# One decoder block on one core: accumulator tiles of one PSUM bank, the scratch write of a transpose on another queue, input sums and chunks at other places, a table loaded later

## The chip, the core and the metric

The kernel runs on one core of one Trainium2 chip. The core has a matrix engine (TensorE, PE in the profile; its weight loads are PEld), a vector engine (VectorE, DVE), an activation engine (ScalarE, ACT), GpSimd (POOL), and a queue processor that only issues transfers (SyncE, SP). They run side by side and wait for each other through semaphores. Matmuls read SBUF and write into banks of the accumulator memory, PSUM, from which DVE and ACT read. Weights come from device memory by DMA. The metric is the device time of one execution in microseconds (us), lower is better; several executions are timed, and one further execution is recorded by the hardware profiler.

## What is computed

One layer on a sequence of 256 tokens of width 2048, all in float32. Cut to what matters:

```python
def swiglu(x, w_gate, w_up, w_down):
    return (jax.nn.silu(x @ w_gate) * (x @ w_up)) @ w_down      # D_FF = 5632
h = x
h = h + 0.5 * swiglu(rms_norm(h, ffn1_norm), ffn1_w_gate, ffn1_w_up, ffn1_w_down)
n = rms_norm(h, mix_norm)
rq, rk, rv, rg, sq, sk, sv = split(n @ w_in)                    # 8 retention heads, 16/2 window heads
ret = silu(rg) * groupnorm(retention(rope(rq), rope(rk), rv))   # two chunks of 128
swa = sliding_window_attention(rope(sq), rope(sk), sv, sinks)   # window 128
h = h + concat(ret, swa) @ w_out
h = h + memory_cross_attention(rms_norm(h, xa_norm), rms_norm(mem, mem_norm), xa_wq, xa_wkv, xa_wo)
h = h + 0.5 * swiglu(rms_norm(h, ffn2_norm), ffn2_w_gate, ffn2_w_up, ffn2_w_down)
out = rms_norm(h, final_norm)
```

## The kernel before

**Data.** The state `h` is held transposed in four tiles `hT[0..3]`, each 128 partitions by 4 x 256 (block b holds rows 512b to 512b+511 of the width, all 256 tokens). A matmul takes 128 tokens of such a block as the stationary operand and 512 columns of a weight as the moving one. Each float32 value is split into a high and a low part (`halves`, lines 80 to 83: ACT copies the high part, line 78, DVE subtracts it, line 83), and a product is three matmuls (`three`, line 644): high by high, high by low, low by high.

**Weights.** A weight piece is 128 x 1024 float32, 512 KB. `load` (lines 356 to 363) issues its DMA on SP into one of `LAND = 10` landing tiles `wf`. `split` turns it into `wh` and `wl`, of which there are four each. A landing tile is free when both halves are made; SP works through its queue in order, and a load whose landing tile is not free yet holds up everything behind it.

**The order of the work** is written out by hand. `all_steps` makes one list. A plain step multiplies one weight piece with one block: two row groups of six matmuls, 12 in all. `run_stream` goes through the list: before a step it runs what has come due (`later(delay, fn)` counts in steps through `clock`; a chunk counts half), splits the pieces of up to `LOOKAHEAD = 3` steps ahead and issues loads of four more. Instructions of due tasks are pinned behind what was issued before them on PE, ACT and DVE; SP keeps the written order throughout.

**Two kinds of unit.** A `Unit` is one 512-column block of a weight, with one accumulator of two banks (`ps_acc`, two tiles of 128 x 2 x 512, one bank for each group of 128 tokens). A `Twin` does two such blocks (gate and up of one feed-forward block b, or two blocks of the down projection). For some of its input blocks (`sevens`: block 3, and also block 2 where b is even; in a down projection the first block of its group) it uses seven products in place of eight, called P1 to P7: six matmuls each, here a chunk. For these the weights are combined first (`prepare`: a subtraction on DVE, line 237, for P5, P6, P7 and P4), and for P5, P6, P3 and P7 so are the inputs (`sums_of`: four scalings on ACT, four additions or subtractions on DVE, line 292, then a split). After the last P1, P5, P6 and P7 the Twin's partial sums are copied from PSUM by ACT and added by DVE (`keep`, `keep_other`, `middle`, `spread`; line 255). Twins take their four banks from the pool `ps_tmp` (four tiles of one bank) and from `ps_acc` (two tiles of two banks) by turns, the first of each feed-forward from `ps_tmp`. The chunks of a Twin lie between the plain steps of the Twin before it; only the first Twin of each feed-forward, b = 1, has none before it, and puts P1, P5, P6, P3, P2, P7 in one row ahead of its own plain steps. `multiply` of any chunk is put into the program after the input sums (`run_until`, line 476).

**First block.** Block b = 0 of each feed-forward is two Units, gate and up. In the first one, the 16 steps of both are interleaved and loaded ahead (`FIRST = 16`). `gate_done` (line 686), when the gate's last step is through, applies Silu and registers the input sums of block 3 (one step later) and block 2 (eight steps later).

**Norms.** `Norm.stat` squares and adds a block; `finish`, `delay` steps after the last block, adds the two halves (line 573), sums over partitions with four tiny matmuls (line 576) and takes the power on GpSimd (line 579).

**Transposes.** `cross` (lines 611 to 630) transposes 32 x 32 squares on DVE into a tile `t4k` (line 618; there are two), writes it to scratch memory `box` with one DMA on SP (line 622, 512 KB), reads it back in four DMAs on GpSimd's queue (line 627, 128 KB each), and `delay` steps later (6 and more) its consumer is put into the program. 64 of these run in all.

**Tables.** `ctab` holds cosines, sines and masks (512 KB) in a tile of its own; it and `sinks` are loaded at step 24. `dmat` takes two landing tiles when the first of the four blocks of the first feed-forward's output is complete (`near_mix`).

Of the kernel before, what the change touches and what calls it, by code (L numbers as in the profile page):

```python
# [34 lines left out]
FIRST = 16  # L35
TURN = 6
SWA_EVERY = 5
LAND = 10
# [5 lines left out]
def decoder_block(ctx: ExitStack, tc: tile.TileContext, a: dict, out: bass.AP):  # L44
# [7 lines left out]
    ps_acc = ctx.enter_context(tc.tile_pool(name="ps_acc", bufs=2, space=bass.MemoryType.PSUM))  # L52
# [17 lines left out]

    def tmp_ps(dt=F32):
        return ps_tmp.tile([P, 512], dt, tag="tmp", name=nm("tmp"))
# [15 lines left out]
    ctab = const.tile([P, C_END], F32, tag="ctab", name="ctab")  # L88
# [94 lines left out]
    class Twin:  # L183
# [16 lines left out]
        def __init__(self, weights, lhs, plain, sevens, sums, done, ahead=False, spare=False):  # L200
            self.w, self.lhs, self.plain, self.sevens = weights, lhs, list(plain), list(sevens)
            self.sums, self.done, self.ahead, self.spare = sums, done, ahead, spare
            self.acc, self.tiles = {}, {}
# [120 lines left out]
    def all_steps():  # L324
        groups = []
        rest = list(units)
        while rest:
# [55 lines left out]
    def run_stream():  # L383
        steps = all_steps()
        steps[:FIRST] = [x for y in zip(steps[: FIRST // 2], steps[FIRST // 2 : FIRST]) for x in y]
        steps[1], steps[2] = steps[2], steps[1]
        loaded, ahead = {}, [FIRST]
        for i in range(0, FIRST, 4):
            if i == 0:
                load_x(0, 0, 2)  # L390
                loaded[0] = loaded[1] = [load(steps[0][0].w[f], 0) for f in range(2)]
                load_x(0, 2, 4)
            else:
                load_x(i // 4, 0, 4)
            for at in range(max(i, 2), i + 4):
                loaded[at] = load(steps[at][0].w, steps[at][3])
# [32 lines left out]
        def multiply_first(u, x, parts, orders):  # L429

            for f, lo, hi in orders:
                for k in range(lo, hi):
                    for t in range(2):
# [3 lines left out]
                            u.acc[t][:, t, f * S : (f + 1) * S], x[:, k, 0, ts], x[:, k, 1, ts], wh, wl,  # L437
# [24 lines left out]
        for at, (u, b, ks, which, first, last) in enumerate(steps):  # L462
# [25 lines left out]
            if first:  # L488
                u.acc = [ps_acc.tile([P, 2, 512], F32, tag="acc", name=nm("acc"))] * 2
                if u.per_half:  # L490
                    u.acc[1] = ps_acc.tile([P, 2, 512], F32, tag="acc", name=nm("acc"))
# [3 lines left out]
            else:  # L495
                for t in range(2):
                    y = (u.acc[t][:, t, : u.n], x, wh, wl, ks, t, first, last)
# [5 lines left out]
            if last:  # L503
                if u.per_half:
                    u.done(u.acc[0], 0)
                    for y in held:
                        by_tokens(*y)
                    u.done(u.acc[1], 1)
                else:
                    u.done(u.acc[0])  # L510
# [100 lines left out]
    def cross(src, then, delay=TURN):  # L611
# [9 lines left out]
        def write():  # L621
            nc.sync.dma_start(box.rearrange("(t p) n -> p t n", t=2), z)
# [24 lines left out]
    def to_h(w, lhs, factor, blocks, norm=None, then=None, spare=0, seven=None, sums=None):  # L647
# [18 lines left out]
        for b in range(4):  # L666
            if seven is None:
                Unit(w, b, 512, lhs, lambda acc, b=b: done([acc[:, t, :] for t in range(2)], b), blocks, pair=True)
# [6 lines left out]
    twins = []  # L675
# [5 lines left out]
    def ffn(norm, w_gate, w_up, down, groups):  # L681
# [4 lines left out]
        def gate_done(b, acc):  # L686
# [29 lines left out]
        twins.clear()  # L716
        starts = [x[0] for x in groups[:2]]
        for g, fbs in enumerate(groups):
            for b in fbs:
# [6 lines left out]
                for f, w in enumerate((w_gate, w_up)):  # L726
                    Unit(w, b, 512, norm.blocks, lambda acc, f=f, done=done: done(f, [acc[:, t, :] for t in range(2)]), range(4), pair=True)
# [588 lines left out]
```

## Time and profile before

| | |
|---|---|
| median of 3 runs | 2197.73 us (2191.67 to 2197.75) |
| profiled execution | 2193.53 us |
| its span, first to last instruction | 2191.7 us |
| mean granted TensorE clock | 0.994 |
| VectorE busy | 1673.9 us, 76% |
| ScalarE busy | 1210.9 us, 55% |
| GpSimd busy | 160.2 us, 7% |
| moved by DMA | 482.62 MB, mean 220 GB/s |

"Busy" is the time in which an engine has an instruction of the program in work; matmuls overlap, so a busy PE is not one at its peak. An engine's wait is put down to the instruction that released it last. The granted clock is the share of full speed at which TensorE was let run.

### The profile page before, as it was taken

The numbers are of one execution on the slowest core, as the hardware profiler recorded it, in microseconds if no ns is written. First come the engines' busy times: TensorE is split into PE (matmuls) and PEld (weight loads), VectorE is DVE, ScalarE is ACT, GpSimd is POOL, SyncE is SP. The second block draws the span as 40 slices with busy tenths as digits, with TensorE's granted clock in tenths as the row PEclk, the third lists the DMA queues.
The fourth block names the chain that finished last, engine by engine and source line by source line (L and its number), as shares of the span: only waits on it lengthen the run. The fifth ranks groups of instructions, "written<-read, shape, count | busy, mean of one in ns | idle before, by whom it ended". The sixth has DMA issues, their size and how long they took to land.

```text
span 2191.7 us, 26751 instructions
## 1 busy us (share of the span) xinstructions
PE 2137.2 (98%) x9564; PEld 1753.1 (80%) x9564; DVE 1673.9 (76%) x1952; ACT 1210.9 (55%) x1519; POOL 160.2 (7%) x273
## 2 busy tenths in 40 slices
PE   9899999999999999999999999998999999999998
PEld 7688777887878888888888888886878778878786
DVE  7987888878976778787765555576988888878875
ACT  6655565555554655546455444355665556555654
POOL 0000000000101100100101100000100000000000
PEclk9999999999999999999999999999999999999999
DMA  6667676867777867666887766585677667666663
GB/s 241 217 220 260 204 233 194 265 203 225 240 220 244 271 192 240 194 201 201 268 240 235 232 216 211 165 255 176 212 250 257 202 188 227 218 215 201 203 234 140
DMA packets 221287, 482.62 MB, mean 220 GB/s; under 512 B 18144, under 2 KB 18144, under 8 KB 221152
## 3 DMA queue, kind: packets, MB, share of 16 engines
q1 hardware_dynamic: 208720, 447.28, 61.8%
q0 software_dynamic: 12288, 33.57, 6.7%
q8 instruction: 75, 1.23, 0.2%
q14 instruction: 60, 0.49, 0.1%
q10 hardware_dynamic: 144, 0.05, 0.0%
HBM read 445.17 MB, written 35.65 MB: 219 GB/s over the span
## 4 chain that ended last, share of the span: by engine, by line
PE 54%; DVE 3%; DMA 3%; issue 1%; ACT 1%; SPq 0%; DVEq 0%; ACTq 0%; POOLq 0%; POOL 0%
PE acc L644 42%; PE tmp L644 11%; DMA wf<-in_ffn_w_up 2%; DVE wl L83 2%; DMA wf<-in_ffn_w_down 1%; PE tmp L877 0%; ACT t2k L78 0%; DVE t2k L698 0%; PE tmp L858 0%; ACT wh L78 0%; DVE t4k L618 0%; DVE tmp L255 0%; DVE blk L83 0%; PE tmp L951 0%; PE tmp L824 0%
## 5 line engine op out<-in xcount | busy, mean ns | idle before, releaser
L644 PE MATMUL acc<-wh,blk 128*128 128x512 f32 (+1 forms) x4336 | 1365.8, 389 | 10.9 <-ACT t2k L78 9.8
L78 ACT ACTIVATE wh<-wf 128x1024 fp32r<-128x1024 f32 (+1 forms) x891 | 929.6, 1054 | 808.4 <-PE acc L644 476.2
L83 DVE TENSOR_TENSOR wl<-wf,wh 128x1024 fp32r<-128x1024 f32 (+1 forms) x891 | 1069.7, 1214 | 380.8 <-ACT wh L78 369.4
L644 PEld LDWEIGHTS acc<-wh,blk 128*128 128x128 f32 x4336 | 813.2, 188 | 185.4 <-ACT t2k L78 15.7
L644 PE MATMUL acc<-wl,blk 128*128 128x512 f32 (+1 forms) x2168 | 841.5, 388 | 0.8 <-DVE wl L83 0.7
L644 PE MATMUL tmp<-wh,blk 128*128 128x512 f32 x1736 | 567.5, 393 | 16.2 <-ACT blk L78 14.4
L644 PEld LDWEIGHTS acc<-wl,blk 128*128 128x128 f32 x2168 | 408.4, 188 | 83.6 <-DVE wl L83 2.8
L644 PEld LDWEIGHTS tmp<-wh,blk 128*128 128x128 f32 x1736 | 328.0, 189 | 88.5 <-ACT blk L78 15.2
L644 PE MATMUL tmp<-wl,blk 128*128 128x512 f32 x868 | 342.6, 395 | 14.5 <-DVE wl L83 14.3
L627 POOL DMA_DIRECT2D t4k<-box x256 | 147.9, 584 | 1812.2 <-DVE wl L83 727.9
L237 DVE TENSOR_TENSOR wf<-wf,wf 128x1024 f32<-128x1024 f32 x152 | 185.1, 1221 | 45.8 <-DMA wf<-in_ffn_w_up 39.7
L644 PEld LDWEIGHTS tmp<-wl,blk 128*128 128x128 f32 x868 | 164.2, 189 | 58.2 <-DVE wl L83 24.3
L618 DVE STREAM_TRANSPOSE t4k<-t2k 128x512 f32<-128x512 f32 x96 | 63.4, 691 | 12.8 <-ACT t2k L78 12.7
L78 ACT ACTIVATE t2k<-acc 128x512 f32<-128x512 f32 x72 | 42.1, 597 | 35.3 <-PE acc L644 22.6
L83 DVE TENSOR_TENSOR blk<-t4k,blk 128x512 fp32r<-128x512 f32 (+2 forms) x72 | 44.1, 653 | 10.7 <-ACT blk L78 10.5
L78 ACT ACTIVATE t2k<-tmp 128x512 f32<-128x512 f32 x68 | 40.4, 594 | 21.6 <-PE tmp L644 19.4
L78 ACT ACTIVATE blk<-t4k 128x512 fp32r<-128x512 f32 (+2 forms) x72 | 39.2, 598 | 5.4 <-DMA t4k<-box 5.3
L78 ACT ACTIVATE blk<-h,gains 128x256 fp32r<-128x256 f32 (+1 forms) x80 | 34.1, 497 | 6.2 <-DVE h L659 4.2
L528 DVE SCALAR_TENSOR_TENSOR blk<-h,gains,blk 128x256 fp32r<-128x256 f32 x64 | 26.7, 478 | 4.0 <-ACT blk L78 4.0
L659 DVE TENSOR_TENSOR h<-h,t4k 128x512 f32<-128x512 f32 x40 | 25.6, 686 | 4.4 <-DMA t4k<-box 4.4
L255 DVE TENSOR_TENSOR acc<-t2k,acc 128x512 f32<-128x512 f32 x42 | 29.0, 690 | 0.0
L255 DVE TENSOR_TENSOR tmp<-t2k,tmp 128x512 f32<-128x512 f32 x42 | 27.7, 689 | 0.5 <-ACT t2k L78 0.5
(136 smaller groups left out, 580.6 us busy)
## 6 DMA issues: line engine op xcount, KB each, us to landing
wf<-in_ffn_w_gate SPq DMA_DIRECT2D x176, 512.0 KB, 5.8
wf<-in_ffn_w_up SPq DMA_DIRECT2D x176, 512.0 KB, 8.4
wf<-in_ffn_w_down SPq DMA_DIRECT2D x176, 512.0 KB, 7.3
box<-t4k SPq DMA_DIRECT2D x64, 512.0 KB, 3.3
t4k<-box POOLq DMA_DIRECT2D x256, 128.0 KB, 7.3
wf<-in_w_in_rqk SPq DMA_DIRECT2D x32, 512.0 KB, 8.2
wf<-in_w_in_rvg SPq DMA_DIRECT2D x32, 512.0 KB, 7.5
wf<-in_w_out SPq DMA_DIRECT2D x32, 512.0 KB, 7.6
```

The costliest lines, as they stand in the source:

```text
L78: return nc.scalar.activation(dst, src, AF.Copy, **kw)
L83: nc.vector.tensor_tensor(lo, src, hi, ALU.subtract)
L237: nc.vector.tensor_tensor(dst, p, q, ALU.subtract)
L255: nc.vector.tensor_tensor(out, a, b, ALU.add)
L528: nc.vector.scalar_tensor_tensor(x[:, k, 1, :], v[:, k, :], g, x[:, k, 0, :], ALU.mult, ALU.subtract)
L618: nc.vector.transpose(z[:, t, :].rearrange("p (g q j) -> p q g j", g=4, q=4), squares_of(v))
L627: nc.gpsimd.dma_start(z[32 * g : 32 * g + 32].rearrange("p t (i n) -> p (t i) n", i=4), far[g])
L644: nc.tensor.matmul(o, x, y, start=first, stop=last, skip_group_check=shared)
L659: nc.vector.tensor_tensor(v, v, out[t], ALU.add)
```

## The change

There are four parts.

1. `ps_acc` has four tiles of one bank in place of two tiles of two. A Unit takes two of them, a Twin all four at once, and the Twins on `ps_tmp` take their four at once too.
2. In `cross`, the write to `box` is issued on GpSimd's queue, as the reads are.
3. The input sums are registered by step, not by `gate_done`. In the first feed-forward those of block 3 start at step 10 and of block 2 at step 14; in the second, 1 and 11 steps after the last block of its input is added. P1 and P5 of the first Twin stand behind the second-last and the last step of block b = 0. `FIRST` is 15, the interleaving of the first 16 steps moves into `all_steps`, and the delay of the second feed-forward's norm is 5.
4. `ctab` has no tile of its own: it takes a landing tile when `near_mix` runs and is loaded there. `LAND` is 11. `sinks` is still loaded at step 24.

```diff
-FIRST = 16
+FIRST = 15
-LAND = 10
+LAND = 11
-    ps_acc = ctx.enter_context(tc.tile_pool(name="ps_acc", bufs=2, space=bass.MemoryType.PSUM))
+    ps_acc = ctx.enter_context(tc.tile_pool(name="ps_acc", bufs=4, space=bass.MemoryType.PSUM))
+    def acc_ps():
+        return ps_acc.tile([P, 512], F32, tag="acc", name=nm("acc"))
-    ctab = const.tile([P, C_END], F32, tag="ctab", name="ctab")
...
         def bank(self, f, t):
-            if self.spare:
-                if (f, t) not in self.acc:
-                    self.acc[f, t] = tmp_ps()
-                return self.acc[f, t]
-            if f not in self.acc:
-                self.acc[f] = ps_acc.tile([P, 2, 512], F32, tag="acc", name=nm("acc"))
-            return self.acc[f][:, t, :]
+            if not self.acc:
+                self.acc = [(tmp_ps if self.spare else acc_ps)() for _ in range(4)]
+            return self.acc[2 * f + t]
...
+        (u, x), (_, y) = groups[:2]
+        x = [z for pair in zip(x, y) for z in pair]
+        groups[:2] = [(u, x[:1] + [x[2], x[1]] + x[3:])]
...
-                    out += u.chunks((P1, P5, P6, P3, P2, P7))
+                    out += u.chunks((P6, P3, P2, P7))
...
+                if isinstance(after, Twin) and not after.ahead and at >= n - 2:
+                    out += after.chunks((P1, P5)[at - n + 2 :][:1])
...
             if first:
-                u.acc = [ps_acc.tile([P, 2, 512], F32, tag="acc", name=nm("acc"))] * 2
-                if u.per_half:
-                    u.acc[1] = ps_acc.tile([P, 2, 512], F32, tag="acc", name=nm("acc"))
+                u.acc = [acc_ps() for _ in range(2)]
...
         def write():
-            nc.sync.dma_start(box.rearrange("(t p) n -> p t n", t=2), z)
+            nc.gpsimd.dma_start(box.rearrange("(t p) n -> p t n", t=2), z)
...
-            if b == 0:
-                for i in range(2):
-                    sums_of(norm, 3 - i, sums, 1 + 7 * i)
...
+        input_sums[norm] = sums
...
+    for b in (3, 2):
+        later(22 - 4 * b, lambda b=b: sums_of(n1, b, input_sums[n1], 0))
...
-    def load_tables():
-        nc.sync.dma_start(ctab, a["ctab"])
-        nc.sync.dma_start(sinks, a["sinks"])
-    later(24, load_tables)
+    later(24, lambda: nc.sync.dma_start(sinks, a["sinks"]))
...
         if b == 0:
+            st["ctab"] = land()
+            nc.sync.dma_start(st["ctab"], a["ctab"])
             st["dmat"] = [land() for _ in range(2)]
...
-    n2 = Norm(G_FFN2, "n2", 4)
+    n2 = Norm(G_FFN2, "n2", 5)
...
         if b == 3:
+            for b in (3, 2):
+                later(31 - 10 * b, lambda b=b: sums_of(n2, b, input_sums[n2], 0))
             for b in range(4):
                 later(19 + 12 * b, lambda b=b: turn_h(b))
```

The other lines of the diff only follow from these: `acc[t]` in place of `acc[:, t, :]`, and `st["ctab"]` in place of `ctab`.

More of the change, by code (lines that the diff above doesn't have):

```diff
@@ L202, in __init__ @@
             self.sums, self.done, self.ahead, self.spare = sums, done, ahead, spare
-            self.acc, self.tiles = {}, {}
+            self.acc, self.tiles = [], {}
             units.append(self)
@@ L384, in run_stream @@
         steps = all_steps()
-        steps[:FIRST] = [x for y in zip(steps[: FIRST // 2], steps[FIRST // 2 : FIRST]) for x in y]
-        steps[1], steps[2] = steps[2], steps[1]
         loaded, ahead = {}, [FIRST]
[L388 to L396, printed above, removed]
+        load_x(0, 0, 2)
+        loaded[0] = loaded[1] = [load(steps[0][0].w[f], 0) for f in range(2)]
+        load_x(0, 2, 4)
+        for at in range(2, FIRST):
+            if at % 4 == 0:
+                load_x(at // 4, 0, 4)
+            loaded[at] = load(steps[at][0].w, steps[at][3])
         ready = {}
@@ L436, in multiply_first @@
                         three(
-                            u.acc[t][:, t, f * S : (f + 1) * S], x[:, k, 0, ts], x[:, k, 1, ts], wh, wl,
+                            u.acc[t][:, f * S : (f + 1) * S], x[:, k, 0, ts], x[:, k, 1, ts], wh, wl,
                             f == 0 and k == 0, False,
@@ L496, in run_stream @@
                 for t in range(2):
-                    y = (u.acc[t][:, t, : u.n], x, wh, wl, ks, t, first, last)
+                    y = (u.acc[t][:, : u.n], x, wh, wl, ks, t, first, last)
                     if u.per_half and t == 1 and at >= len(steps) - TAIL:
@@ L504, in run_stream @@
                 if u.per_half:
-                    u.done(u.acc[0], 0)
+                    u.done(u.acc, 0)
                     for y in held:
                         by_tokens(*y)
-                    u.done(u.acc[1], 1)
+                    u.done(u.acc, 1)
                 else:
-                    u.done(u.acc[0])
+                    u.done(u.acc)
         run_until(lambda: not tasks)
@@ L667, in to_h @@
             if seven is None:
-                Unit(w, b, 512, lhs, lambda acc, b=b: done([acc[:, t, :] for t in range(2)], b), blocks, pair=True)
+                Unit(w, b, 512, lhs, lambda acc, b=b: done(acc, b), blocks, pair=True)
             elif b % 2 == 0:
@@ L726, in ffn @@
                 for f, w in enumerate((w_gate, w_up)):
-                    Unit(w, b, 512, norm.blocks, lambda acc, f=f, done=done: done(f, [acc[:, t, :] for t in range(2)]), range(4), pair=True)
+                    Unit(w, b, 512, norm.blocks, functools.partial(done, f), range(4), pair=True)
                 if norm is not n1:
@@ L770, in rope @@
         c, s1, s2 = (
-            ctab[:, at + t * 64 : at + t * 64 + w].rearrange("p (o d) -> p o d", o=1).broadcast_to([P, nh, w])
+            st["ctab"][:, at + t * 64 : at + t * 64 + w].rearrange("p (o d) -> p o d", o=1).broadcast_to([P, nh, w])
             for at, w in ((C_COSS, 64), (C_SINS, 32), (C_SINS + 32, 32))
@@ L781, in scaled @@
         x = t2k()
-        copy(x[:, :n], acc[:, t, :n], scale=norm.scale(t))
+        copy(x[:, :n], acc[t][:, :n], scale=norm.scale(t))
         return x
@@ L818, in swa_group @@
         sv3 = s.rearrange("p (n k) -> p n k", n=nh)
-        mask = ctab[:, C_MASK + S - nkey : C_MASK + S].rearrange("p (o k) -> p o k", o=1).broadcast_to([P, per, nkey])
+        mask = st["ctab"][:, C_MASK + S - nkey : C_MASK + S].rearrange("p (o k) -> p o k", o=1).broadcast_to([P, per, nkey])
         if t == 1:
@@ L826, in swa_group @@
                     )
[L827 removed]
+            mask = st["ctab"][:, C_MASK : C_MASK + S].rearrange("p (o k) -> p o k", o=1).broadcast_to([P, nh, S])
             nc.vector.scalar_tensor_tensor(sv3, ps, 64 ** -0.5, mask, ALU.mult, ALU.add)
@@ L925, in finish @@
                 if "rot" not in st:
-                    st["rot"] = ctab[:, C_COSR : C_COSR + 512].rearrange("p (c s) -> p c s", c=2)
+                    st["rot"] = st["ctab"][:, C_COSR : C_COSR + 512].rearrange("p (c s) -> p c s", c=2)
                     nmix.spread_over(st["rot"])
@@ L945, in finish @@
                         later(3 + i // 2, lambda i=i: ret_scores(g, i, qk))
-            cross([acc[:, t, :] for t in range(2)], finish, TURN + 1)
+            cross(acc, finish, TURN + 1)
         return done
@@ L998, in done @@
                 sg = t2k()
-                nc.scalar.activation(sg, acc[:, t, :], AF.Silu, scale=nmix.scale(t))
+                nc.scalar.activation(sg, acc[t], AF.Silu, scale=nmix.scale(t))
                 nc.vector.tensor_tensor(ret[t], ret[t], sg, ALU.mult)
@@ L1082, in done @@
             for t in range(2):
-                copy(v[:, 0, t, :], acc[:, t, :], scale=nmem.scale(t))
+                copy(v[:, 0, t, :], acc[t], scale=nmem.scale(t))
                 nc.vector.scalar_tensor_tensor(
-                    v[:, 1, t, :], acc[:, t, :], nmem.scale(t), v[:, 0, t, :], ALU.mult, ALU.subtract
+                    v[:, 1, t, :], acc[t], nmem.scale(t), v[:, 0, t, :], ALU.mult, ALU.subtract
                 )
@@ L1183, in ffn2_down @@
             else:
-                Unit(w, nb, 512, acts, lambda acc, nb=nb: done(nb, [acc[:, t, :] for t in range(2)]), fbs)
+                Unit(w, nb, 512, acts, functools.partial(done, nb), fbs)
             if nb == 1:
@@ L1207, in very_last @@
         for c in range(2):
-            hs = add_down(acc[:, t, c * S : (c + 1) * S], t, 1536 + c * S, S)
+            hs = add_down(acc[t][:, c * S : (c + 1) * S], t, 1536 + c * S, S)
             squares(parts[:, t, 3 + c : 4 + c], hs)
```

3 lines of the change are left out of this document (1 added, 2 removed).

## The prediction

> **What bounds it now.** I read the page's first part, then PE's waits, the granted clock in stretches, and the timeline around the longest waits.
>
> ```profile
> span 2191.7 us, 26751 instructions
> PE 2137.2 (98%) x9564; PEld 1753.1 (80%) x9564; DVE 1673.9 (76%) x1952; ACT 1210.9 (55%) x1519; POOL 160.2 (7%) x273
> ```
>
> PE is busy for all but 2191.7 - 2137.2 = 54.5 us of the span, and the change removes no matmul. What it can win is inside these 54.5 us, plus what PE loses at a lowered clock while it counts as busy. The view of PE's waits over the whole span divides the idle time (in all, times, longest):
>
> ```profile
> PE tmp L644 <- ACT blk L78: 14.4, 2, 7.8
> PE tmp L644 <- DVE wl L83: 14.3, 19, 2.0
> PE acc L644 <- ACT t2k L78: 9.8, 14, 0.8
> PE tmp L576 <- DVE t2k L573: 2.2, 2, 1.8
> PE tmp L101 <- POOL ident masks.py:199: 1.4, 1, 1.4
> PE tmp L644 <- ACT wh L78: 1.3, 3, 0.5
> PE acc L644 <- ACT wh L78: 1.2, 2, 0.9
> PE acc L644 <- DVE wl L83: 0.7, 2, 0.4
> ```
>
> These eight make 45.3 us; nearly all else is the start and the end of the span, which stay. The first row is two waits for the first Twins' input sums, one in each feed-forward. The second is weight halves that come late. The third is fourteen waits on an accumulator. The same view for 640 to 1480 us, where attention and the projections run, has three rows, 1.5 us together:
>
> ```profile
> PE acc L644 <- ACT t2k L78: 0.7, 1, 0.7
> PE acc L644 <- DVE wl L83: 0.4, 1, 0.4
> PE tmp L576 <- DVE t2k L573: 0.4, 1, 0.4
> ```
>
> So there is nothing to win in that third of the run, only to lose. After its long waits PE also runs slowly. Of each stretch here the columns are length, busy time (and count) of each engine, granted clock, DMA share, GB/s:
>
> ```profile
> 62.00:68.20 6.20, 6.16 (x15) 4.33 (x16) 2.45 (x3) 2.20 (x4) 1.46 (x3) 0.52 1.01 274
> 1486.00:1491.40 5.40, 4.71 (x16) 3.80 (x17) 1.95 (x4) 0.00 (x0) 1.63 (x1) 0.68 0.29 98
> 1513.10:1519.00 5.90, 5.90 (x14) 4.35 (x15) 3.39 (x3) 1.91 (x3) 2.33 (x4) 0.53 1.00 308
> ```
>
> At clock 0.52 a stretch of 6.2 us loses 6.2 x 0.48 = 3.0 us; the others lose 5.4 x 0.32 = 1.7 and 5.9 x 0.47 = 2.8.
>
> **Part 1, single banks.** At 121 us a Twin from `ps_acc` goes from its last chunk to its plain steps; at 155 us one from `ps_tmp` does the same.
>
> ```profile
> 119.85 0.39 PE L644 MATMUL acc<-wh,blk 128*128 128x512 f32 x1
> 120.93 0.50 PE L644 MATMUL acc<-wh,blk 128*128 128x512 f32 x1 [0.69 <-ACT t2k L78]
> 121.27 0.40 PE L644 MATMUL acc<-wl,blk 128*128 128x512 f32 x1
> 120.28 0.60 ACT L78 ACTIVATE t2k<-acc 128x512 f32<-128x512 f32 x1 [0.30 <-PE acc L644]
> 155.26 0.60 ACT L78 ACTIVATE t2k<-tmp 128x512 f32<-128x512 f32 x1 [0.25 <-PE tmp L644]
> 155.29 0.39 PE L644 MATMUL tmp<-wl,blk 128*128 128x512 f32 x1
> 155.51 0.61 PE L644 MATMUL tmp<-wh,blk 128*128 128x512 f32 x2
> ```
>
> P7 has just written bank (0,1) and ACT copies it; the plain step writes bank (0,0). With both in one tile PE waits for the copy, with a tile for each bank it runs on: matmuls keep coming every 0.22 us. The delay is more than the gap: starts 119.85 to 120.93 to 121.27 are 1.08 and 0.34 us apart where 0.22 would do, so one such wait costs 0.86 + 0.12 = 0.98 us, with the restart behind the idle 0.69. The mean of the fourteen is the same (9.8 / 14 = 0.70): 14 x 0.98 = 13.7 us. All fourteen name `acc`. After the copy the bank's own next matmul is a row group later (6 x 0.22 = 1.3 us against 0.60), so no wait takes the place. Bounds: 12 and 14.
>
> **Part 2, the write on GpSimd, with the eleventh landing tile.** First SP's waits (whole span), DVE's wait for pieces, and SP at 320 us:
>
> ```profile
> SPq L362 <- DVE wl L83: 706.7, 332, 9.2
> SPq L622 <- DVE t4k L618: 606.8, 59, 26.9
> DVE wf L237 <- DMA wf<-in_ffn_w_up: 39.7, 17, 4.6
> 321.57 0.37 SPq L362 DMA_DIRECT2D wf<-in_ffn_w_gate  x1
> 332.08 0.37 SPq L622 DMA_DIRECT2D box<-t4k  x1
> 334.52 4.77 SPq L362 DMA_DIRECT2D wf<-in_ffn_w_up  x5
> ```
>
> 59 of 64 writes hold SP for 606.8 / 59 = 10.3 us each, because SP reaches them before DVE has transposed. From 321.57 to 332.08 no load is issued, and then they come in a burst; behind such bursts DVE stands still for pieces (39.7 us in 17 waits) and PE gets its low halves late. These are the rows `wl` and `wh`: 14.3 + 0.7 + 1.3 = 16.3 us in 24 waits, and with the restart of 0.98 - 0.69 = 0.29 us for each, 16.3 + 7.0 = 23.3 us. With the write gone from SP a load is held by landing tiles alone, and there is one more. Not all goes: in the stretches with two `sevens` blocks up to eight pieces lie waiting to be combined, and DVE has little room. I take three quarters, 17 us; bounds 6 (only waits behind a burst shorten, and DVE is late anyway) and 22.
>
> What GpSimd pays: one issue more for each of 64 crosses. The nearest rows are its reads and both landing times, min/median/max, of SP's write and of the reads:
>
> ```profile
> L627 POOL DMA_DIRECT2D t4k<-box x256: 582/582/745, 61.0 to 2126.2; - x128
> DMA to landing us min/median/max: 2.8/3.3/7.4
> DMA to landing us min/median/max: 2.6/7.3/10.2
>   ACT blk L78: 7.4, 4
>   DVE h L659: 4.4, 5
> ```
>
> GpSimd is 7% busy, so 64 x 0.58 = 37 us there cost nothing by themselves. Queued behind the write are its reads, which need it anyway, and now and then a norm's power. The trace has no write from this queue: its landing lies between 2.6 and 10.2 us, where SP's takes 3.3. I take 5, nearest the reads' middle less a share for the bursts that now end. The reads were made slow by the burst SP let go just after each write, so they may win back as much. Consumers wait for reads today in the last two rows, nine times, 11.8 us; PE has up to three steps in hand there (3 x 12 x 0.22 = 7.9 us) and waits little. Only the norms' sums hang on a cross directly. I charge 2 us, with bounds of 10 lost and 2 won.
>
> **Part 3, earlier sums.** Before, the two first Twins cost 14.4 us of idle and 3.0 + 2.8 = 5.8 of slow clock, 20.2 us. Sums made ahead end that wait. What is late next is DVE. Its groups from 47 to 71 us:
>
> ```profile
> L83 DVE TENSOR_TENSOR wl<-wf,wh 128x1024 fp32r<-128x1024 f32 x7 | 8.5, 1218 | 5.7 <-ACT wh L78 5.7
> L237 DVE TENSOR_TENSOR wf<-wf,wf 128x1024 f32<-128x1024 f32 x4 | 4.9, 1221 | 0.1
> L292 DVE TENSOR_TENSOR blk<-blk 128x256 f32<-128x256 f32 x4 | 1.5, 417 | 0.0
> L698 DVE SCALAR_TENSOR_TENSOR t2k<-acc,n,t2k 128x512 f32<-128x512 f32 x2 | 1.4, 744 | 0.0
> L618 DVE STREAM_TRANSPOSE t4k<-t2k 128x512 f32<-128x512 f32 x2 | 1.3, 686 | 0.0
> ```
>
> From P5's subtraction until P7 can start, DVE has five splits (6.1), three subtractions (3.7), the up result (1.4), its transposes (1.3) and, in the first feed-forward, now block 2's sums (1.5 + 1.2): 15.2 us, and about 2 more of waits for ACT's high halves, as some of the 5.7 show. PE meanwhile has the last gate and up steps and P1, P5, P6, P3, P2: 2 x 12 + 5 x 6 = 54 matmuls, 11.9 us. So some 5 us stay there, in two or three short waits. In the second feed-forward block 2's sums fall behind P7: 12.5 + 2 against 11.9, so about 3. Win 20.2 - 8 = 12 us; bounds 4 (each remaining wait brings slow clock again) and 18.
>
> The norm's delay of 5 moves its tiny matmuls one step (12 x 0.22 = 2.6 us) past a wait of 1.8 and its 1.7 us of slow clock, but block 3's sums (2.7 us of DVE) now stand ahead of the addition that they need. I take 1.5; bounds -2 and 3.5.
>
> [...]
>
> **Part 4, `ctab`.** It is the same 512 KB, loaded later, in the stretch with 1.5 us of waits; from there to the last rotary use eleven tiles less three leave eight, as ten less two did. Nothing.
>
> **Sum.** 13.7 + 17 - 2 + 12 + 1.5 = 42 us. The profiled execution took 2193.53 us, of which the span is all but 2 us: 2151.5. It was 4.2 us under the median of the runs shown (2197.73), and the same 42 from that gives 2155.7; I say 2153, between them.
>
> **Rivals.** *DVE takes over* (0.15). Pieces come early, but in the chunk stretches DVE has more to do than PE, so late halves stay. For it: 15.2 against 11.9 above. Against: DVE stands idle 39.7 us for pieces in those very stretches. Then part 2 gives 6, part 3 gives 4, the norm 0: 13.7 + 6 - 2 + 4 = 22, about 2172 us; with the bounds of the cross at their worst, within 0.3%.
>
> *The single banks do nothing* (0.04), if PE waits on the copy for another reason. Against: fourteen of fourteen on `acc`, and at 155 us none on `tmp`. Then 42 - 14 = 28, about 2166 us.
>
> *The writes on GpSimd make crosses late* (0.08), slower than before. DVE's instructions would hold up GpSimd's issue, and transfers from its queue are slow: with the 10.2 us of the slowest read in place of 3.3, a cross is 6.9 us longer. Place: the nine consumers that wait today and the two norms. If PE's hand covers only about 2 us, 11 x (6.9 - 2) = 54 us are lost against 42 + 2 won elsewhere: about 2204 us. It decides from 2 + 44 / 11 = 6.0 us per cross; below that it is faster or the same. For it: no slack at these nine. Against: an issue took 582 ns at the median and 745 at most beside a DVE that is 76% busy, and reads were slowed by bursts that end.
>
> [...]
>
> **Chances and range.** My forecast has 0.73. Faster by over 0.3% (6.6 us, about what a measurement of this kernel can tell from no change): 0.73 + 0.12 + 0.04 = 0.89. Same: 0.03 of the first rival and 0.03 of the last, 0.06. Slower: 0.05. All low bounds together give 12 + 6 - 10 + 4 - 2 = 10 us, all high ones 14 + 22 + 2 + 18 + 3.5 = 59.5; not all fall on one side, so I go from 18 to 59 off the profiled time: 2135 to 2176.
>
> **What would show it.** The row `acc <- ACT t2k` is gone or nearly. SP no longer waits for L618, and DVE's wait for `in_ffn_w_up` falls under 10 us. The wait for `ACT blk` at the first Twins becomes short waits for `wl` with at most one slow stretch each. A write lands in about 5 us, and the reads under 7.3. Wrong would be: waits for `wl` as long as before with DVE never idle, or new waits of PE between 640 and 1480 us.

## The result, and the profile after

| | before | after |
|---|---|---|
| median | 2196.07 us (2191.67 to 2197.75, 4 runs) | 2177.47 us (2169.46 to 2178.52, 4 runs) |
| ratio after / before | | 0.991, 95% interval 0.9882 to 0.9939 |
| profiled execution | 2193.53 us | 2177.1 us |

The change wins 18.6 us by the medians; the prediction said 42 off the profiled time, and 2177 lies just above its range. Below, a gain in us is (1 - ratio) x 2193 with the interval worked out in the same way: here 20 us, 13 to 26. A later measurement of the same kernel, e17, gave 2170.88 us (below the 2174 to 2180 expected of it), ratio 0.9911 (0.9893 to 0.9929): 19.5 us, 16 to 23. This closer one is used from the experiments on.

First lines of the page of after:

```profile
span 2175.3 us, 26666 instructions
PE 2132.3 (98%) x9564; PEld 1758.9 (81%) x9564; DVE 1674.5 (77%) x1952; ACT 1212.3 (56%) x1517; POOL 208.0 (10%) x337
```

PE is idle for 2175.3 - 2132.3 = 43.0 us in place of 54.5. Line numbers have moved: the matmul of `three` is L641, the copy of `copy` L81, the subtraction for low halves L86, the one in `prepare` L235, the write to `box` L619, its reads L624, the addition to `h` L656, the norm's finish L570 and L573. PE's waits over the whole span (in all, times, longest):

```profile
PE tmp L641 <- DVE wl L86: 8.9, 6, 2.6
PE tmp L641 <- ACT wh L81: 8.0, 10, 2.6
PE tmp L573 <- DVE t2k L570: 5.7, 2, 3.0
PE acc L641 <- DVE wl L86: 3.8, 4, 1.2
PE acc L641 <- ACT wh L81: 2.0, 4, 1.0
```

The fourteen waits of `acc` for `ACT t2k` are gone, and so are the two long ones for the input sums. But waits for halves, which were to fall to a quarter, are now 8.9 + 8.0 + 3.8 + 2.0 = 22.7 us in 24 waits, where they were 17.5 in 26 (the prediction's 16.3 in 24 left out its row of 1.2, `acc <- ACT wh`). Of the 22.7, 9.6 lie at the two first Twins, where the forecast itself left about 8; the other 13.1 stand where about 4 were forecast. SP's largest wait, two of DVE's, and the transfers' medians (KB each, us from issue to landing):

```profile
SPq L365 <- DVE wl L86: 1190.1, 514, 10.6
```
```profile
DVE h L656 <- DMA t4k<-box: 21.8, 5, 5.4
DVE wf L235 <- DMA wf<-in_ffn_w_up: 10.5, 6, 5.6
```
```profile
box<-t4k POOLq DMA_DIRECT2D x64, 512.0 KB, 3.9
t4k<-box POOLq DMA_DIRECT2D x256, 128.0 KB, 6.2
```

SP no longer waits for the transposes (L615), DVE's wait for pieces fell from 39.7 to 10.5 us, the write lands in 3.9 and the reads in 6.2. All of this was forecast, but for the wait for pieces, which was to fall under 10. New is the first DVE row: additions to `h` wait 21.8 us for reads of `box`, where they waited 4.4. And between 640 and 1480 us, where PE waited 1.5 us in all, it now waits 7.0, which the prediction had named as a sign of being wrong:

```profile
PE tmp L573 <- DVE t2k L570: 2.7, 1, 2.7
PE acc L641 <- DVE wl L86: 2.1, 2, 1.2
PE tmp L641 <- DVE blk L86: 1.1, 1, 1.1
PE tmp L947 <- DVE t2k L952: 1.1, 1, 1.1
```

At the first Twin of the first feed-forward, PE's waits (45 to 73 us), the stretch at half clock behind them, and DVE's timeline (start, us, engine, line):

```profile
PE tmp L641 <- DVE wl L86: 2.4, 1, 2.4
PE tmp L641 <- ACT wh L81: 2.1, 2, 1.8
PE tmp L641 <- ACT t2k L81: 1.8, 1, 1.8
PE acc L641 <- DVE wl L86: 0.9, 1, 0.9
```
```profile
65.30:72.10 6.80, 4.54 (x10) 3.27 (x11) 6.52 (x8) 3.73 (x6) 1.28 (x3) 0.50 0.99 271
```
```profile
49.30 1.22 DVE L235 TENSOR_TENSOR wf<-wf,wf 128x1024 f32<-128x1024 f32 x1
...
62.44 3.49 DVE L235 TENSOR_TENSOR wf<-wf,wf 128x1024 f32<-128x1024 f32 x3
65.85 1.22 DVE L86 TENSOR_TENSOR wl<-wf,wh 128x1024 fp32r<-128x1024 f32 x1
66.98 0.69 DVE L253 TENSOR_TENSOR tmp<-t2k,tmp 128x512 f32<-128x512 f32 x1
```

The sums are early, but from P5's subtraction at 49.30 to the end of the addition that P7 needs, at 67.67, DVE takes 18.4 us. There are five subtractions of pieces (L235) in it, where the prediction counted three. PE loses 7.2 us in waits, and at half clock it is busy for 4.54 us, which costs 4.54 x 0.50 = 2.3: 9.5, not much less than the one long wait had cost (7.8 + 3.0). The same sum for the first Twin of the second feed-forward is 4.9 us of waits and 1.7 of slow clock, 6.6.

### The profile page after: what moved, and what is told of

It is laid out like the page before. It is cut to its first block, busy times and chain, and to the rows that moved or that the text cites. A ratio compares the mean times of both kernels' runs of the same rounds, so it can differ in the third digit from the quotient of the medians.

```text
span 2175.3 us, 26666 instructions
## 1 busy us (share of the span) xinstructions
PE 2132.3 (98%) x9564; PEld 1758.9 (81%) x9564; DVE 1674.5 (77%) x1952; ACT 1212.3 (56%) x1517; POOL 208.0 (10%) x337
## 3 DMA queue, kind: packets, MB, share of 16 engines
q0 software_dynamic: 21504, 67.13, 11.4%
## 5 line engine op out<-in xcount | busy, mean ns | idle before, releaser
L81 ACT ACTIVATE wh<-wf 128x1024 fp32r<-128x1024 f32 (+1 forms) x891 | 929.0, 1053 | 803.6 <-PE acc L641 453.0
L86 DVE TENSOR_TENSOR wl<-wf,wh 128x1024 fp32r<-128x1024 f32 (+1 forms) x891 | 1068.7, 1215 | 395.6 <-ACT wh L81 382.9
L641 PE MATMUL acc<-wh,blk 128*128 128x512 f32 (+1 forms) x4336 | 1366.4, 389 | 2.0 <-ACT wh L81 2.0
L641 PEld LDWEIGHTS acc<-wh,blk 128*128 128x128 f32 x4336 | 815.6, 189 | 171.8 <-ACT wh L81 4.4
L641 PE MATMUL acc<-wl,blk 128*128 128x512 f32 (+1 forms) x2168 | 842.9, 389 | 3.8 <-DVE wl L86 3.8
L641 PE MATMUL tmp<-wh,blk 128*128 128x512 f32 x1736 | 567.6, 392 | 10.4 <-ACT wh L81 8.0
L641 PEld LDWEIGHTS acc<-wl,blk 128*128 128x128 f32 x2168 | 409.6, 189 | 87.1 <-DVE wl L86 5.7
L641 PEld LDWEIGHTS tmp<-wh,blk 128*128 128x128 f32 x1736 | 327.1, 189 | 83.4 <-ACT wh L81 12.5
L641 PE MATMUL tmp<-wl,blk 128*128 128x512 f32 x868 | 340.2, 392 | 8.9 <-DVE wl L86 8.9
L641 PEld LDWEIGHTS tmp<-wl,blk 128*128 128x128 f32 x868 | 163.9, 189 | 46.1 <-DVE wl L86 11.8
L235 DVE TENSOR_TENSOR wf<-wf,wf 128x1024 f32<-128x1024 f32 x152 | 182.8, 1220 | 13.5 <-DMA wf<-in_ffn_w_up 10.5
L619 POOL DMA_DIRECT2D box<-t4k x64 | 46.6, 728 | 1463.4 <-DVE t4k L615 1411.6
L624 POOL DMA_DIRECT2D t4k<-box x256 | 149.2, 589 | 282.8 <-DMA box<-t4k 196.8
L615 DVE STREAM_TRANSPOSE t4k<-t2k 128x512 f32<-128x512 f32 x96 | 64.7, 695 | 5.8 <-ACT t2k L81 5.7
L81 ACT ACTIVATE t2k<-acc 128x512 f32<-128x512 f32 x72 | 43.1, 598 | 26.3 <-PE acc L641 19.3
L86 DVE TENSOR_TENSOR blk<-t4k,blk 128x512 fp32r<-128x512 f32 (+2 forms) x72 | 44.2, 653 | 9.8 <-ACT blk L81 9.7
L81 ACT ACTIVATE t2k<-tmp 128x512 f32<-128x512 f32 x68 | 40.3, 593 | 20.4 <-PE tmp L641 13.1
L81 ACT ACTIVATE blk<-h,gains 128x256 fp32r<-128x256 f32 (+1 forms) x80 | 34.1, 496 | 18.1 <-DVE h L656 16.2
L81 ACT ACTIVATE blk<-t4k 128x512 fp32r<-128x512 f32 (+2 forms) x72 | 39.1, 595 | 7.1 <-DMA t4k<-box 7.1
L656 DVE TENSOR_TENSOR h<-h,t4k 128x512 f32<-128x512 f32 x40 | 25.8, 686 | 21.8 <-DMA t4k<-box 21.8
```

Of the source, the lines that this page charges most:

```text
L81: return nc.scalar.activation(dst, src, AF.Copy, **kw)
L86: nc.vector.tensor_tensor(lo, src, hi, ALU.subtract)
L235: nc.vector.tensor_tensor(dst, p, q, ALU.subtract)
L615: nc.vector.transpose(z[:, t, :].rearrange("p (g q j) -> p q g j", g=4, q=4), squares_of(v))
L619: nc.gpsimd.dma_start(box.rearrange("(t p) n -> p t n", t=2), z)
L624: nc.gpsimd.dma_start(z[32 * g : 32 * g + 32].rearrange("p t (i n) -> p (t i) n", i=4), far[g])
```

## The experiments

Two theories stood at the start. The first is the prediction's own accounting, which added up the parts. The second, **theory 1**, comes from the two traces: the single banks win what was forecast; the GpSimd queue wins early loads, and loses them to late crosses; the earlier sums win little, since DVE's work is the bound at the first Twins.

### Each part alone

e1, single banks (the hunks with `acc_ps` and `u.acc`); e2, the write on GpSimd with ten landing tiles; e3, sums and chunks earlier; e4, `ctab` in a landing tile, with eleven of them:

```diff
e2 -nc.sync.dma_start(box...    +nc.gpsimd.dma_start(box...
e3 +later(22 - 4 * b, lambda b=b: sums_of(n1, b, input_sums[n1], 0))   (and FIRST, all_steps, n2)
e4 -LAND = 10  +LAND = 11       -ctab = const.tile(...)  +st["ctab"] = land()
```

> The kernel before with part 1 alone (accumulator tiles of one bank). Both theories agree: the fourteen waits of PE on the copy (9.8 us, with restarts 13.7) vanish and nothing takes their place, 12 to 14 us faster than before. If the time falls by less than 8 us, PE was held there by something else, and the theory that the rest of the change gained only about 5 us falls too.

> The kernel before with part 2 alone (scratch writes issued on GpSimd, ten landing tiles). Theory 1, from the two traces: SP's loads come early and most waits for weight halves go (about 14 us won), but where two crosses follow each other within 10 us the second write stands behind the first one's reads in GpSimd's queue and on the DMA rings, lands after 7 to 10 us, and VectorE waits 4 to 5 us for it at about five places (10 to 12 us lost): in all 0 to 6 us faster, with VectorE's wait for the read back near 20 us. Rival, the prediction's accounting: about 15 us faster, with that wait below 8 us.

> The kernel before with part 3 alone (input sums by step, P1 and P5 ahead, norm delay 5). Theory 1: the first Twins are held by the amount of VectorE work up to the first plain step, which part 3 does not lessen, and the second norm's small matmuls now wait longer: between 2 us slower and 3 us faster than before. Rival, the prediction's accounting: 12 + 1.5 = 13.5 us faster, and the change lost it through the writes on GpSimd.

> The kernel before with part 4 alone (rotary table in a landing tile, eleven landing tiles). Theory 1: pieces still come in bursts behind SP's writes, one tile more shortens the waits for halves a little: 1 to 5 us faster. Rival: nearly all of what was won on weight halves comes from the eleventh tile, about 10 us faster. The prediction counted it together with part 2.

| | median | ratio (interval) | gain, us |
|---|---|---|---|
| e1 | 2165.63 | 0.9872 (0.9853 to 0.9890) | 28 (24 to 32) |
| e2 | 2189.72 | 0.9987 (0.9968 to 1.0005) | 3 (-1 to 7) |
| e3 | 2189.42 | 0.9979 (0.9970 to 0.9988) | 5 (3 to 7) |
| e4 | 2186.65 | 0.9965 (0.9952 to 0.9978) | 8 (5 to 11) |

(The kernel before, beside them: 2194.31.) By the unrounded ratios they make 43 us together, the forecast sum, but of other terms, and the whole change wins half of it. e1 alone beats the whole change, and its gain is twice what both theories expected. e2 is where theory 1 put it, with 24.3 us of DVE's waits for reads of `box`. e3 wins more than theory 1 allowed, but far less than 13.5; e4 lies between its two expectations, nearer the rival. PE's waits for halves in e1:

```profile
PE tmp L641 <- DVE wl L86: 6.4, 8, 1.8
PE acc L641 <- DVE wl L86: 3.3, 2, 1.7
PE acc L641 <- ACT wh L81: 1.1, 1, 1.1
```

The fourteen waits are gone as forecast, and the late halves fell too, from 17.5 us to 11 (a row of 0.2 not shown), though the writes of `box` still stand in SP's queue. Two questions followed: why the banks win twice their price, and what takes it back.

### Why the single banks win 28 us

ScalarE's waits to copy a finished accumulator, before and in e1:

```profile
ACT t2k L78 <- PE acc L644: 43.7, 57, 2.9
```
```profile
ACT t2k L81 <- PE acc L641: 28.0, 74, 0.8
```

Theory 2: with two banks in one tile ScalarE's copy of the first half waited for PE's matmuls into the second, and this wait cost the rest. e5 brings that wait back with single banks:

```diff
-for t in range(2):
+for t in reversed(range(2)) if last and not u.per_half else range(2):   (and so in Twins from ps_acc)
```

> The single banks alone, but in the last step of a unit PE multiplies the second half of the tokens first and the first half last, so that ScalarE, which copies the first half first, again waits for both, as it did with two banks in one tile; the work is the same. Theory 2: the single banks won 28.7 us instead of 13.7 because a tile of two banks held ScalarE too: its copy of a finished half waited for PE's matmuls into the other half (31 waits of over 1 us before, 4 with the single banks), and all that stands behind it in ScalarE's queue, the high halves of the weights, came late. Then the fourteen waits of PE stay away, ScalarE's waits of over 1 us come back (over 20 of them), and of the 15 us beyond the fourteen waits most is lost again: 2175 to 2182 us. Rival: the 15 us come from another order of ScalarE's and VectorE's work that the scheduler found with four tiles free: then the time stays at 2163 to 2169 us.

Measured: 2167.46 us beside 2193.85, ratio 0.9882 (0.9866 to 0.9898), 26 us. The waits came back,

```profile
ACT t2k L81 <- PE acc L641: 44.1, 57, 3.5
```

and the time did not, which speaks against theory 2. It does not settle it, because e5's order of instructions is not e1's: by the traces at least 74 of VectorE's places differ. For within one engine the order of the program is not the written one; the toolchain's scheduler lays it out at compile time. With the false dependencies gone, 244 of VectorE's 1952 instructions, 56 of ScalarE's and 177 of TensorE's stood at another place in e1 than before. **Theory 3**: the order wins the rest. e9 holds the order of before on TensorE, VectorE and ScalarE with explicit dependencies, e10 that of e1 on VectorE and ScalarE alone (`ORDERS` lists, for each engine, which instruction of the written program stands at each place):

```diff
+for engine, text in ORDERS.items():
+    ...
+    ins = made[engine][at + int(shift)]
+    if prev is not None:
+        order(prev, ins)
```

> The single banks alone, but TensorE's, VectorE's and ScalarE's instructions are held in the order in which they stand in the kernel before. The scheduler, which sees that the banks no longer depend on each other, had moved 244 of VectorE's 1952 instructions and 56 of ScalarE's 1461 to other places. Theory 3: this other order is where the 15 us beyond the fourteen waits come from. Then 2176 to 2183 us, with the waits for the copy gone and 14 to 18 us of waits for late halves as before. Rival (the tiles themselves, by waits of ScalarE or VectorE that end): the order does not matter, 2163 to 2169 us.

> The kernel before with its tiles of two banks, but VectorE's and ScalarE's instructions held in the order that the single banks gave them. Theory 3 (the order is worth about 15 us): 2175 to 2184 us, with the fourteen waits for the copy still there (about 10 us of idle) and late halves down to 10 us or so. Rival (the order is worth nothing without the single banks): 2190 to 2198 us.

e9: 2176.36 us beside 2192.61, ratio 0.9916 (0.9898 to 0.9933); e10: 2184.18, 0.9955 (0.9938 to 0.9973). In us won:

| | order of before | order of e1 |
|---|---|---|
| tiles of two banks | 0 | 10 (6 to 14), e10 |
| single banks | 18 (15 to 22), e9 | 28 (24 to 32), e1 |

The two are additive: tiles 18, order 10. No kernel was held in its own order, which would show what the holding itself costs; that 18 and 10 make the 28 leaves little room for such a cost. PE's waits in e9 (those for halves) and in e10 show each of them:

```profile
PE tmp L707 <- DVE wl L134: 12.9, 15, 2.2
PE acc L707 <- ACT wh L129: 1.4, 3, 1.0
PE acc L707 <- DVE wl L134: 1.1, 1, 1.1
PE tmp L707 <- ACT wh L129: 0.9, 3, 0.5
```
```profile
PE acc L702 <- ACT t2k L118: 9.8, 14, 0.8
PE tmp L702 <- DVE wl L123: 7.8, 10, 1.8
PE acc L702 <- DVE wl L123: 3.0, 4, 0.9
PE tmp L702 <- ACT wh L118: 1.6, 5, 0.5
```

In e9 the fourteen waits are gone and the halves are late as before (16.3 us in 22 waits); in e10 the fourteen are back to the tenth of a microsecond, and the halves are late for less (13.4 us in 20 waits, with a row of 1.0 not shown). Theory 3 is shown, with some two thirds of the size it expected. Theory 2 keeps at most the 4 us by which the tiles win more in the old order than the 13.7 of the fourteen waits.

### What takes it back

> Parts 1 and 4 together, the write on SP's queue and the sums where they were. By itself the first won 28.7 us and the other 7.7. Theory 1 (they shorten different waits, PE's for banks and DVE's for pieces): about 2158 us, 2154 to 2162. Rival (both live off the same 16 us of late halves, of which the single banks already took most): 2162 to 2167 us.

> The whole change but with the crosses' writes on SP's queue as before. Theory 1 (the queue gives back what the rest wins: second crosses land 4 to 5 us later and PE stops in attention, at both norms and at the second feed-forward's start): about 2160 us, 2154 to 2165, and no wait of VectorE for box reads over 2 us. Rival (the earlier sums give it back, by filling DVE where halves are late): 2172 to 2180 us.

> The whole change but with the sums of the input made after the first Twins' steps, as before. Theory 1 (the queue is the loss, the sums are worth at most 5 us): 2177 to 2183 us, with the long wait for the sums (7.8 us) back and the late crosses still there. Rival (the earlier sums are the loss): 2155 to 2168 us.

> Parts 1 and 3 together, the write on SP's queue, ten landing tiles and the rotary table loaded at the start. By itself part 1 won 28.7 us and part 3 won 4.9; parts 1, 3 and 4 together won 30.7. If they add up: about 2160 us, 2157 to 2163, and the eleventh landing tile then costs or gives nothing in this company. Rival (the earlier sums need the eleventh tile, whose pieces come sooner): 2165 to 2170 us.

| | median | beside | ratio (interval) | gain, us |
|---|---|---|---|---|
| e6, parts 1, 4 | 2167.77 | 2193.85 | 0.9883 (0.9868 to 0.9898) | 26 (22 to 29) |
| e12, parts 1, 3 | 2165.93 | 2192.61 | 0.9874 (0.9855 to 0.9893) | 28 (23 to 32) |
| e7, parts 1, 3, 4 | 2163.19 | 2193.85 | 0.9863 (0.9846 to 0.9879) | 30 (27 to 34) |
| e8, parts 1, 2, 4 | 2175.75 | 2193.85 | 0.9917 (0.9898 to 0.9936) | 18 (14 to 22) |

On top of the single banks neither the tables (e6) nor the sums (e12) give anything that these intervals tell from none; both times are those of the rivals, 0.8 us over the range in e6. Both kernels with part 2 are behind their like without it, e8 behind e6 by 7 us (2 to 13) and the whole change behind e7 by 10 (5 to 16). So theory 1 holds against its rivals in e7 and e8, though not in every number: e8 is 1 us under its range, and in e7 the longest wait of VectorE for reads of `box` is 2.7 us, where 2 was the limit. The whole change without the queue, e7, has the lowest median of all, and by the ratios 10 us less than the whole change; e1, e6, e12, e13 and e14 are not told from it.

Its crosses were the suspect. e11 lets 11 of the 64, those that follow another within five steps, write from SP's queue:

```diff
+near = clock[0] - st.get("crossed", -9) < 5
+st["crossed"] = clock[0]
-nc.gpsimd.dma_start(box...
+(nc.sync if near else nc.gpsimd).dma_start(box...
```

> The whole change, but 11 of the 64 crosses, those that come less than five steps after another, write from SP's queue as before; the other 53 write from GpSimd's. Theory 1 (only a write that stands behind the reads of the cross ahead of it in GpSimd's queue is late): most of the 14 us that the queue costs come back, 2162 to 2168 us, and no cross takes over 17 us from its transposes to the landing of its reads. Rival (every cross is 1 to 1.5 us longer from that queue, and it is the single ones before the norms and in attention that cost): 2171 to 2178 us.

2174.99 us beside 2192.61, 0.9908 (0.9890 to 0.9927), 20 us: the rival's time, though only 2 of the 64 crosses still take over 17 us (longest 19.1). But the comparison with e7 is one of two orders as well (271 of VectorE's instructions stand elsewhere in the whole change than in e7), so the next runs hold the order. e13 is the whole change and e14 is e11, both in e7's order:

> The whole change, writes on GpSimd's queue, but TensorE's, VectorE's and ScalarE's instructions held in the order that they have in the kernel of e7 (the whole change with the writes on SP's queue); the scheduler had put 271 of VectorE's instructions at other places between the two. Theory 4 (the order that comes with the queue is what costs): 2160 to 2167 us, near e7's 2163. Theory 1 (the late crosses cost, whatever the order): 2172 to 2180 us, near the whole change's 2177. Anything between divides the 14 us.

> As the run before, with e7's order, and the 11 crosses that follow another closely write from SP's queue, the other 53 from GpSimd's. Theory 4: as e13, 2158 to 2166 us. Theory 1 with all its cost in second crosses: 2160 to 2166 us while e13 stays at 2172 to 2180. If both stay over 2170, the single crosses from GpSimd's queue cost it.

e13: 2165.76 us beside 2192.87, 0.9869 (0.9851 to 0.9887), 29 us (25 to 33); e14: 2166.87, 0.9873 (0.9857 to 0.9889), 28. So the whole change is 9 us (4 to 15) faster when nothing but the order is put back, and then not to be told from e7: theory 4 holds. e14 against e11 says the same, 8 us (2 to 13). And e14 against e13, in one order, shows no gain from taking the 11 writes off GpSimd's queue. What kind of move it is, the first Twin shows. In e13 DVE (its `prepare` is L279, its additions L297) makes two subtractions there, and the third comes behind P7's additions:

```profile
62.32 2.35 DVE L279 TENSOR_TENSOR wf<-wf,wf 128x1024 f32<-128x1024 f32 x2
...
72.19 1.29 DVE L297 TENSOR_TENSOR tmp<-t2k,tmp 128x512 f32<-128x512 f32 x2 [1.63 <-ACT t2k L125]
...
74.52 1.22 DVE L279 TENSOR_TENSOR wf<-wf,wf 128x1024 f32<-128x1024 f32 x1
```

In the whole change all three stand at 62.44, ahead of the split and the addition, and PE's wait of 1.8 for `ACT t2k` comes from there; e13 has none. But this place is only an example of the move: e13 waits 1.3 us more there for a low half, and the whole change loses only 0.4 us of its 9 there. By the starts of the same matmuls in the two traces the 9 us come in many small steps: 3.7 up to 777 us, 2.0 in the middle, 3.5 from 1530 us on. Subtractions that stand earlier are most of the difference between the two orders on VectorE. A likely reason is that the scheduler, with no write of `box` in SP's queue, counts pieces as there sooner; this is only argued.

How much of the forecast gain the queue itself has was left for two runs, each in the order of the kernel that it is compared with:

> Part 2 alone (the write on GpSimd's queue, ten landing tiles), with TensorE's, VectorE's and ScalarE's instructions held in the order of the kernel before. With the scheduler's own order this part gave 4.6 us. Theory 4 (moved early, the subtractions of pieces push the splits back, and that ate what the freed loads won): 2176 to 2184 us, 9 to 17 won. Rival (freed loads win little in any order, because the late crosses take it back): 2186 to 2192 us.

> Parts 1 and 2, held in the order that part 1 alone has (2165.6 us, 28.7 won). Theory 4: the queue gives what it gives in e15 or a part of it, 2155 to 2166 us. Rival (the queue takes as much by late crosses as it wins by early loads, and nothing is left to win after the single banks): 2166 to 2172 us.

> The whole change once more, in the scheduler's own order, beside the others on one chip: 2174 to 2180 us by all theories, 17 to 20 under the kernel before; it is there to narrow the interval on which the share of the order (whole change in its own order against e13) rests.

e15: 2196.32 us beside 2192.77, 1.0015 (1.0000 to 1.0031): 3 us lost (0 to 7), 4 us over even the rival's range. e16: 2170.06, 0.9904 (0.9889 to 0.9919): 21 us, 7 behind e1 (2 to 12). e17 is told above. Theory 4's forecast falls in both: in one and the same order the queue wins nothing. Nor does the order that comes with the queue always cost: part 2 alone is 6 us (1 to 11) better in its own order (e2) than in that of before (e15). Where the time goes shows when the matmuls with the numbers 1, 3401 and 6801 and the last, 9564, start in each trace. The first stretch (to 793 us in before) is the first feed-forward and its output with the first projections; the second (to 1538) attention and the memory part; the third the second feed-forward. Their lengths in us:

```
             write on    1 to 3401   to 6801   to 9564
before       SP            791.7      745.1     644.6
e15          GpSimd        780.3      767.8     638.2
e1           SP            778.3      740.5     632.7
e16          GpSimd        778.5      755.2     627.4
e7           SP            773.7      742.9     631.1
e14          53 GpSimd     773.5      749.4     631.7
e13          GpSimd        775.5      753.4     627.1
after        GpSimd        779.2      755.4     630.6
```

In the order of before, e15 wins 11.4 us in the first stretch and 6.4 in the third, together 17.8, and loses 22.7 in the second. With single banks there is less to win: over the first and the third stretch e16 wins 5.1 us against e1, and e13 2.2 against e7, while they lose 14.7 and 10.5 in the second. So the second stretch has the same sign in each pair of one order: it is 740 to 745 us with the writes on SP, 753 to 768 with all of them on GpSimd, and between them with 53. From the end of a cross's transposes to the landing of its last read, 10 of e15's 64 crosses take over 17 us (longest 22.0), 10 of after's, 11 of e13's, 2 of e14's, and none of before's (longest 16.5). Late second crosses are not the whole loss, then: e14 has next to none, and its second stretch is still 6.5 us longer than e7's. PE's waits in e15 between 640 and 1500 us:

```profile
PE tmp L646 <- DVE t2k L643: 8.1, 2, 4.8
PE acc L714 <- DVE wl L135: 5.2, 4, 2.3
PE tmp L714 <- DVE blk L135: 2.9, 1, 2.9
```

These 16.2 us lie at four places, from 811, 1059, 1278 and 1490 us on. Ahead of each ScalarE or VectorE waits 3 to 7 us for reads of `box`, and behind each the clock is at half (0.50 to 0.51) for 3.5 to 6.9 us, 24.0 us in all. PE is busy for 20.5 of them, which at half clock cost 10.3: with the waits 26.5, and 21.5 when what before lost in this stretch (5 us) is taken off, nearly the 22.7. By the starts of the same matmuls the four places lose 3.0, 9.0, 5.6 and 5.1 us. At the second and the third the late reads are those of a cross that follows another within 8 us, and land 7 us later than in before; at the first and the last they are those of a cross by itself, and land about 1 us later. The second place, in chosen rows of GpSimd, DVE and PE (write L692, reads L697), and the stretch behind it:

```profile
1035.65 2.34 POOL L697 DMA_DIRECT2D t4k<-box  x4 [6.29 <-DMA box<-t4k]
1037.98 0.72 POOL L692 DMA_DIRECT2D box<-t4k  x1
1047.68 2.32 POOL L697 DMA_DIRECT2D t4k<-box  x4 [8.98 <-issue]
```
```profile
1056.93 1.29 DVE L729 TENSOR_TENSOR h<-h,t4k 128x512 f32<-128x512 f32 x2 [6.88 <-DMA t4k<-box]
1059.41 0.50 PE L714 MATMUL acc<-wl,blk 128*128 128x512 f32 x1 [2.27 <-DVE wl L135]
1065.75 1.01 PE L646 MATMUL tmp<-ones,t2k 128*128 128x1 f32 x4 [3.32 <-DVE t2k L643]
```
```profile
1065.40:1072.30 6.90, 6.55 (x18) 5.31 (x18) 1.60 (x3) 0.60 (x1) 1.42 (x3) 0.51 0.85 285
```

Two blocks of the projection finish close together. The second write is issued right behind the first's reads and lands 9.2 us later; only then are its own reads issued. The addition to `h` needs them, stands at the head of DVE's queue for 6.88 us, and holds a split and then the norm: PE stops twice, 5.6 us, and runs at half clock behind it, which costs 6.55 x 0.49 = 3.2 us more.

## Why the prediction was wrong

**Part 1** ("14 x 0.98 = 13.7"): right in mechanism, too low in size, above its own bound of 14. All fourteen waits went, and in the order of before the tiles are worth 18 us (15 to 22); where the 4 us over the 13.7 come from is not shown. What it did not see are 10 us from the scheduler's new order.

**Part 2** ("17 us" of late halves, crosses charged "2 us, with bounds of 10 lost and 2 won"): this step failed. The first term holds by itself when the order is held, 17.8 us in e15, but on top of the single banks only 5.1 and 2.2 us of it are left (e16, e13). The charge was mis-sized: 22.7 us in e15, 14.7 and 10.5 in e16 and e13. It relied on PE's steps in hand, and did not look at two crosses in a row, in which the write of one stands behind the reads of the other (14.6 of e15's 22.7 us), nor at the half clock behind each stop. The 5 us for a landing were close at the median (3.9) and said nothing of these. The third rival named the effect, late crosses, and its place, the consumers without slack and the norms; its 54 us took eleven places to lose 4.9 us each, and it was four that lost 3 to 9 with the half clock. That DVE holds up GpSimd's issue, as it supposed, is not shown: in after, beside a DVE that is 77% busy, a read took 585 ns to issue at the median and 614 at most, a write 724 and 883.

**Part 3** ("20.2 - 8 = 12 us; bounds 4 ... and 18"): 5 us alone (e3), none to 4 on top of others. The step that failed is what was to stay, "some 5 us" and "about 3": in after 9.5 and 6.6 stay, since DVE took 18.4 us, PE stopped five times instead of two or three, and the clock went to half behind it, for which only the low bound had left room. 20.2 - 9.5 - 6.6 leaves 4 us. The first rival had this term right, with its 4, and its time, 2172, is the nearest. That is luck: it has 13.7 for part 1, which alone gave 28, and 6 - 2 for part 2, which alone gave nothing clear. And by e13 some 9 us of what it put down to a full DVE are the order. The norm's delay was to win 1.5; the row `L573 <- DVE t2k L570` rose from 2.2 to 5.7 us. Late crosses are only a part of that: in e3, with the writes on SP, the row is at 3.8 already.

The clock stood low behind short waits too. In before it was at 0.68 over the 5.4 us from 1486 us on, where a wait of 1.8 us ends; in after it was at 0.51 for 3.5 us behind a wait of 2.60 us, PE's only one from 296 to 312 us (PE's timeline, then start and end, length, busy times, clock):

```profile
309.64 0.50 PE L641 MATMUL tmp<-wl,blk 128*128 128x512 f32 x1 [2.60 <-DVE wl L86]
```
```profile
311.00:314.50 3.50, 3.50 (x10) 2.73 (x9) 3.26 (x4) 2.53 (x4) 0.00 (x0) 0.51 0.47 150
```

**Part 4** ("Nothing"): 8 us alone (e4). Most likely it is the eleventh landing tile, which the prediction had booked under part 2: DVE's wait for `in_ffn_w_up` fell from 39.7 to 32.9 us there. But e4 changed the order of instructions too, and the two were not taken apart. On top of the banks nothing clear is left of it.

**The sum** failed beside its terms. Alone the parts win 43 us, together 20: on top of part 1, parts 3 and 4 give nothing clear (e6, e12) and part 2 loses 7 us (e16 against e1). That parts 2, 3 and 4 live off the same late halves, of which e1 leaves 11 us, is likely, but not shown. And each part changed the scheduler's order of instructions also where it touches nothing, for better (part 1, 10 us) or worse (the whole change, 9 us).

What stays open: which of the moved instructions cost the time (only whole orders were tried), and how the 10 us between the whole change and e7 divide. By the ratios 9 (4 to 15) are the order and 1 (-4 to 7) the queue; by the single traces, 9 and 8, with e7's trace 3 us under its median. e7 held in the order of the whole change, which would tell, was not run.

## What to carry to other kernels

Put independent accumulators into tiles of their own: in this framework the tile, not the bank, is what others wait for (fourteen waits, 9.8 us, with two banks in a tile; none with one). Where a scheduler lays out the instructions, compare the order of two builds before an edit is credited with a gain, and hold the order to measure the edit. A transfer moved from a busy queue to an idle one is not priced by its median landing alone (3.9 us here, and 9.2 behind another cross's reads): look at what stands ahead of it there when two come in a row, and at the consumers that have no slack.

## What was not expected of the hardware

A write of 512 KB from GpSimd's queue took 728 ns to issue, where the four reads of 128 KB took 589 each (rows below, of after), and landed in 3.9 us at the median against 3.3 from SP's; behind the reads of another cross, as at 1037.98 us in e15, it took 9.2. Loads of 512 KB from SP's queue landed sooner once the writes were gone from it: by the page's last part the medians of the large weights, 5.8 to 8.4 us before, were 4.6 to 5.4 in e15, which has the same order.

```profile
L619 POOL DMA_DIRECT2D box<-t4k x64 | 46.6, 728 | 1463.4 <-DVE t4k L615 1411.6
L624 POOL DMA_DIRECT2D t4k<-box x256 | 149.2, 589 | 282.8 <-DMA box<-t4k 196.8
```
